# Pads in SBUF and three reorderings in a two-layer diffusion backbone

## The chip, the core and the metric

The kernel runs on one core of one Trainium2 chip, as one program. The metric is the device time of one execution in microseconds (us). The kernel before is known from three timed runs and from one more execution that was profiled.

## What is computed

The reference is one inference step of a hybrid backbone: two layers over 128 context tokens and 256 latent tokens of width 1024, all in float32. Each layer is a half-step SwiGLU FFN, a mixer, and a second half-step FFN.

```python
def _ffn_sublayer(x, shift, scale, gate, w1, w3, w2, g, b):
    y = _swiglu(_modulate(x, shift, scale), w1, w3, w2)
    return _layernorm(ALPHA * x + 0.5 * gate * y, g, b)
...
def _merge(h, y_f, y_m, y_n, p):
    g_f, g_m, g_n = jnp.split(jax.nn.sigmoid(h @ p['w_gate'] + p['b_gate']), 3, axis=-1)
    return (g_f * y_f + g_m * y_m + g_n * y_n) @ p['w_out']
```

The mixer projects the modulated input `h` by `w_in` into the inputs of three branches: a Fourier branch (`y_f`), latent attention (`y_m`) and neighbourhood attention (`y_n`). Beside the two token outputs the program returns the caches of the context tokens, among them the new neighbourhood keys (`new_na_k`) of both layers.

## The kernel before

**Numbers as pairs.** Every float32 operand of a product is held as a high and a low part in the reduced type fp32r, and `mm3` (line 327) issues three matmuls for each product: high by high, high by low, low by high. The weights come from HBM by SP's DMAs into `raw` tiles; ScalarE (ACT) casts them to `whi` (line 188) and VectorE (DVE) subtracts to get `wlo` (line 193).

**Memory.** There are two kinds of SBUF tiles. `fixed` tiles are placed once, in the order of the calls at the start of `run` (line 1231): the modulated activations `hm` (high part `hmh`, low part `hml`), the identity `ident`, and small ones. All larger working tiles are `slot`s, 26 of 4096 bytes and 22 of 3072 bytes to a partition, which stand behind the fixed tiles and are used again and again: `raw`, `whi`, `wlo`, the hidden activations `sT`, the queries and keys, the softmax rows `pr`, the residual rows `z`. Since 4096 and 3072 are multiples of 128, all slots start at one residue modulo 128 bytes.

**Stages.** The tokens are three tiles of 128. In an FFN `body` (line 1368) 22 hidden chunks `j` pass one after the other: for each, 48 matmuls of 384 columns make `w1` and `w3` (24 each; the profile calls both `w`), with weights as the stationary operand and `hm` as the moving one. Then 18 matmuls of 512 columns of `second` (line 1359) add an older chunk into the six output banks `y`; there the stationary operand is `sT` and the moving one a weight slot. The last eight chunks are kept for `tail` (line 1401), which adds them tile by tile, so that the layer norm of a tile (`residual`, line 538) goes on beside the matmuls of the next. The first chunks of the next stage (`head`: `hd` in an FFN; `uq`, `kv`, `uf` in a mixer) have `hm` as the stationary and the weights as the moving operand; so have the values `nv`.

**The mixer** (`mixer_body`, line 939) computes the neighbourhood queries and keys (`nq`, `nk`: weights stationary, `hm` moving, as in `w`), copies the context tokens' keys into `kf`, transposes these on TensorE into the bank `nkO`, copies that to `ko` and stores it from POOL's queue (lines 1142 to 1147). After that `attention` (line 846) runs over eight heads: scores `s` of two heads at a time, a filler piece (a gate chunk `g` of 24 matmuls and a branch chunk `yb` of 12), the transposes `pa` and `pb` of the head before, and the product with the values `o` (`attn_pv`, line 822) of the head before that.

**Order.** SP's queue is ordered by a planner from counted matmul columns. On the other engines the instructions follow the source within a scheduler's limits; each engine then runs its own queue in order and waits at semaphores.

The end of the program is the last call of `transition` (line 598): for the last tile the eight kept chunks are added to columns 0 to 511 and then to columns 512 to 1023; `residual` scales each half, adds `x`, takes the statistics, normalises and stores.

Of the kernel before, what the change touches and what calls it, by code (L numbers as in the profile page):

```python
# [8 lines left out]
F32 = mybir.dt.float32  # L9
F32R = mybir.dt.float32r  # L10
AF = mybir.ActivationFunctionType
ALU = mybir.AluOpType
# [4 lines left out]
P = 128  # L17
D = 1024
KD = 8
DEPTH = 2  # L20
NT = 3
TOK = 384
D_FF = 2816
NCH = D_FF // P
# [7 lines left out]
ALPHA = (2.0 * DEPTH) ** 0.25  # L32
# [56 lines left out]
class Kernel:  # L89
# [261 lines left out]
    def stats(self, x):  # L351
        nc = self.nc
        st = self.small(12)
        for h in range(2):
            nc.vector.bn_stats(out=st[:, h * 6:h * 6 + 6], in_=x[:, h * 512:h * 512 + 512])
        mv = self.small(2)
        nc.vector.bn_aggr(out=mv, in_=st.rearrange("p (a b) -> p a b", a=2))
        return mv


# [177 lines left out]
    def residual(self, t, ys, rows, f, last=None):  # L538
        nc = self.nc
        gate = rows[0 if t == 0 else 1]  # L540
        z = self.slot([P, D], F32, "z")
        sm = self.small(3)
        for h in range(2):
            c = slice(h * 512, h * 512 + 512)
            nc.vector.scalar_tensor_tensor(out=z[:, c], in0=ys[h], scalar=f, in1=gate[:, c], op0=ALU.mult, op1=ALU.mult)
            nc.vector.scalar_tensor_tensor(out=z[:, c], in0=self.x[t][:, c], scalar=ALPHA, in1=z[:, c], op0=ALU.mult, op1=ALU.add,
                                           accum_out=sm[:, h:h + 1])
        if last:
            mv = self.stats(z)
            r = self.rstd(mv[:, 1:2], 1.0, 1e-5)  # L550
            for h in range(2):
                c = slice(h * 512, h * 512 + 512)
                nc.vector.scalar_tensor_tensor(out=z[:, c], in0=z[:, c], scalar=mv[:, 0:1], in1=rows["ln_g"][:, c], op0=ALU.subtract, op1=ALU.mult)
            for h in range(2):
                c = slice(h * 512, h * 512 + 512)
                nc.vector.scalar_tensor_tensor(out=z[:, c], in0=z[:, c], scalar=r, in1=rows["ln_b"][:, c], op0=ALU.mult, op1=ALU.add)
                last(t, z, c)
            return
        st, _ = self.sumsq(z, sm[:, 0:1], sm[:, 1:2])
        r = self.rstd(st[:, 1:2], 1.0 / D, 1e-5)  # L560
        nc.vector.scalar_tensor_tensor(out=z, in0=z, scalar=st[:, 0:1], in1=rows["ln_g"], op0=ALU.add, op1=ALU.mult)
        nc.vector.scalar_tensor_tensor(out=z, in0=z, scalar=r, in1=rows["ln_b"], op0=ALU.mult, op1=ALU.add,
                                       accum_out=sm[:, 2:3])
        self.x[t], self.xsum[t] = z, sm[:, 2:3]
# [33 lines left out]
    def transition(self, prev, nxt, mod):  # L598
        n = {}
        if prev is None:  # L600
            with self.tc.manual_schedule(engines={mybir.EngineType.PE, mybir.EngineType.Activation, mybir.EngineType.DVE}):
                self.begin(nxt)
            return

        def res(t):
            self.residual(t, prev.ys[t], prev.rows(t), 0.5, prev.store if nxt is None else None)

        def norm(t):
            if nxt is not None:
                n[t] = self.normed(t)  # L610

        def modu(t):
            if nxt is not None:
                self.modulate(t, n.pop(t), self.mod[mod])

        tl = [prev.tail(t) for t in range(NT)]
        for p in tl[0]:
            p()
        res(0)
        norm(0)  # L620
        for p in tl[1]:
            p()
        cut = prev.cut
        if cut == 0:
            modu(0)
        a = self.ev
        res(1)
        for i, p in enumerate(tl[2]):
            if cut and i == cut:
                modu(0)  # L630
            p()
        norm(1)
        self.quiet.append((a, self.ev, HUSH[mod[1]] if mod else 0))
        if nxt is None:
            res(2)
            return
        late = LATE[mod[1]]

        def last():
            norm(2)  # L640
            if mod[1] == 1:
                for t in range(NT):
                    self.spill(mod[0], t)

        if late < 2:
            res(2)
        if late < 1:
            last()
        self.inhead = True
        hd = [nxt.head(t) for t in range(NT)]  # L650
        for t in range(2):
            at = (M1, M2)[t][mod[1]]
            for p in hd[t][:at]:
                p()
            modu(t + 1)
            if t == 0 and late > 1:
                res(2)
            if t == 0 and late > 0:
                last()
            for p in hd[t][at:]:  # L660
                p()
        for p in hd[2]:
            p()
        self.inhead = False
# [157 lines left out]
    def attn_pv(self, pt, v, h, oT):  # L822
        nc = self.nc
        o = self.psum("o")
        for oc, kts in ((slice(P, TOK), (1, 2, 3)), (slice(0, P), (0,))):
            for kt in kts:
                pc = slice(kt * 256 - 256, kt * 256) if kt else slice(768, 896)
                for y in range(2):
                    nc.tensor.matmul(o[:, oc], lhsT=v[kt][:, h].rearrange("p a b -> p (a b)"), rhs=pt[y][:, pc],
                                     start=kt == kts[0] and y == 0, stop=kt == kts[-1] and y == 1)  # L830
        if h % 2 == 0:
            self.oz = self.slot([P, TOK], F32, "oz")
        z = self.oz[h % 2 * 64:h % 2 * 64 + 64]
        nc.scalar.copy(out=z, in_=o[64:128, 0:TOK])
        nc.vector.tensor_tensor(out=z, in0=o[0:64, 0:TOK], in1=z, op=ALU.add)
        if h % 2:
            ot = self.slot([P, 2, TOK], F32R, "oT")
            self.split(ot[:, 0], ot[:, 1], self.oz)
            oT.append(ot)
# [99 lines left out]
    def mixer_body(self, ph):  # L939
        nc, I, K, O, l = self.nc, self.I, self.K, self.O, ph.l  # L940
# [91 lines left out]
        w = self.ukv(l, 0)  # L1032
        for pr in range(4):
            b = self.psum("kn")
            for kc in range(2):
                lhs = tuple(x[:, kc, 2 * pr:2 * pr + 2].rearrange("p a b -> p (a b)") for x in w)
# [5 lines left out]
        w = self.ukv(l, 1)  # L1042
        vm = []
        for t in range(4):
            b = self.psum("v")
# [35 lines left out]
        vn = []  # L1081
# [16 lines left out]
        oM = []  # L1098
# [25 lines left out]
        for p2 in range(4):  # L1124
            for nme in ("nq", "nk"):
# [10 lines left out]
                else:  # L1136
# [2 lines left out]
                    self.split(kk[:, 0, TOK:512], kk[:, 1, TOK:512], pk[:, p2 * P:(p2 + 1) * P])  # L1139
                    kN.append(kk)  # L1140
                    nc.vector.tensor_copy(out=kf[:, p2], in_=b[:, 0:P])
        po = self.psum("nkO")
        for p2 in range(4):
            nc.tensor.transpose(po[:, p2 * P:(p2 + 1) * P], kf[:, p2], self.ident)
        ko = self.slot([P, 512], F32, "ko")
        nc.scalar.copy(out=ko, in_=po)
        nc.gpsimd.dma_start(out=O[4][0, l].rearrange("a h j -> a (h j)"), in_=ko)

        early = {}

# [15 lines left out]
        def gate_early(d):  # L1166
            def go():
                early[d] = self.gate_chunk(l, 2, d, True)
            return go
# [9 lines left out]
            return x  # L1179

        oN = []
        self.attention(sc_na, 2, vn, oN, [acc_piece(1, d, oM) for d in range(KD)] + [gate_early(0), gate_early(1)])
        mT = []
        for d in range(KD):
            self.ada_flush()
# [45 lines left out]
    def run(self):  # L1231
        nc, I, K, O = self.nc, self.I, self.K, self.O

        self.hm = (self.fixed([P, KD, TOK], F32R, "hmh"), self.fixed([P, KD, TOK], F32R, "hml"))
        self.ident = self.fixed([P, P], F32, "ident")
        make_identity(nc, self.ident)
        self.mhalf = self.fixed([P, 1], F32, "mhalf")
        nc.vector.memset(self.mhalf, -0.5)
        self.mask = self.fixed([P, 64], F32, "mask")
# [38 lines left out]
class FFN:  # L1278
# [77 lines left out]
                k.split(st[:, 0], st[:, 1], b[:, 0:TOK])  # L1356
                self.sT[2 * g + a] = st

    def second(self, j, ts, start, stop, ns=range(2)):
        k = self.k  # L1360
        w2 = k.W(("w2", self.l, self.f, j), f"ffn{self.f}_w2", self.l, j * P, 1, 0, D)
        for t in ts:
            for n in ns:
                c = slice(n * 512, n * 512 + 512)
                lhs = tuple(self.sT[j][:, hl, t * P:(t + 1) * P] for hl in range(2))
                k.mm3(self.ys[t][n], lhs, tuple(w[:, 0, c] for w in w2), start, stop)

    def body(self):
        k, nc = self.k, self.k.nc
# [28 lines left out]
            self.second(q, range(NT), q == 0, False)  # L1398
        self.pend = pend

    def tail(self, t):
        def piece(j, ns):
            return lambda: self.second(j, [t], False, j == NCH - 1, ns)
        return [piece(j, [n]) for n in range(2) for j in self.pend]


class Mixer:
# [14 lines left out]
    def body(self):  # L1422
        self.k.mixer_body(self)

    def tail(self, t):
        k, l = self.k, self.l

        def piece(n, c):
            def go():
                if t not in self.ys:  # L1430
                    self.ys[t] = [k.psum("wo") for _ in range(2)]
                self.out(t, n, c)
            return go
        return [piece(n, c) for n in range(2) for c in range(KD)]
# [88 lines left out]
```

## Time and profile before

| quantity | value |
|---|---|
| median of 3 runs | 1880.86 us (1880.1 to 1881.82) |
| profiled execution | 1881.5 us |
| its span, first to last instruction | 1879.7 us |
| PE (TensorE) busy | 1853.3 us, 99% of the span |
| DVE busy | 1406.2 us, 75% |
| ACT busy | 786.9 us, 42% |
| POOL busy | 95.6 us, 5% |

The profiled execution lies 0.64 us over the median, and 1.8 us of it are outside the span. Matmuls are pipelined: the duration that the profile gives a single one (339 ns for one `w` of 384 columns) overlaps that of the next. The pace at which they follow each other is therefore read from a piece of the chain of waits, where so many matmuls of one kind stand with their common time: 48 in 8.48 us are 176.7 ns each. [...]

### The profile page before, as it was taken

How to read it: one execution, taken by the hardware profiler on the slowest of the kernel's cores; microseconds unless marked ns; L12 is line 12 of the kernel's file. 1: busy time of each engine (PE TensorE's matmuls, PEld its weight loads, DVE VectorE, ACT ScalarE, POOL GpSimd, SP SyncE). 2: the span in 40 equal slices, each digit the busy share in tenths (PEclk: the TensorE clock that was granted, in tenths of full speed). 3: DMA queues.
4: the chain of work that ended last, by engine and by line, in shares of the span. 5: the costliest groups of instructions: out<-in, count | busy, mean ns of one | idle time of the engine just before them, and what ended most of it. 6: DMA issues, size and time to landing. Idle time of an engine off the chain costs nothing. (4 is left out here: it accounts for less than half of the span.)

```text
span 1879.7 us, 27219 instructions
## 1 busy us (share of the span) xinstructions
PE 1853.3 (99%) x10555; PEld 1737.3 (92%) x10555; DVE 1406.2 (75%) x2190; ACT 786.9 (42%) x1312; POOL 95.6 (5%) x115
## 2 busy tenths in 40 slices
PE   7999999999999999999999999999999999999998
PEld 5899998999899999999999999999999998999996
DVE  5688888689887677888877878978798776533345
ACT  4433335456355453333353333355553553433330
POOL 0000002000100010000000000120001000000000
PEclk9999999999999999999999999999999999999999
DMA  9866656234735346666545666552365354344422
GB/s 302 279 217 211 211 201 212 88 100 125 226 106 196 123 146 217 197 224 210 193 150 189 223 215 214 191 163 88 113 197 152 112 194 138 118 134 123 145 91 79
DMA packets 225858, 320.22 MB, mean 170 GB/s; under 512 B 33040, under 2 KB 182144, under 8 KB 225600
## 3 DMA queue, kind: packets, MB, share of 16 engines
q1 hardware_dynamic: 223616, 313.89, 52.2%
q0 software_dynamic: 2112, 4.59, 0.6%
q8 instruction: 83, 1.36, 0.3%
q14 instruction: 47, 0.39, 0.1%
HBM read 312.32 MB, written 8.02 MB: 170 GB/s over the span
## 5 line engine op out<-in xcount | busy, mean ns | idle before, releaser
L193 DVE TENSOR_TENSOR wlo<-raw,whi 128x1024 fp32r<-128x1024 f32 (+4 forms) x420 | 490.6, 1185 | 156.2 <-ACT whi L188 73.9
L188 ACT CAST whi<-raw 128x1024 fp32r<-128x1024 f32 (+4 forms) x420 | 420.4, 1021 | 326.4 <-DVE wlo L193 83.7
L77 PE MATMUL w<-hmh,whi 128*128 128x384 f32 x1152 | 390.6, 339 | 0.8 <-ACT sl L77 0.8
L77 PE MATMUL w<-hmh,wlo 128*128 128x384 f32 x1152 | 389.6, 338 | 0.0
L77 PE MATMUL w<-hml,whi 128*128 128x384 f32 x1152 | 389.6, 338 | 0.0
L77 PE MATMUL y<-whi,sT 128*128 128x512 f32 x1056 | 336.7, 391 | 0.9 <-DVE sT L77 0.6
L77 DVE SCALAR_TENSOR_TENSOR acc<-raw,cs,acc 128x1024 f32<-128x1024 f32 x236 | 294.7, 1281 | 28.7 <-DMA raw<-in_w_ada_dram 28.5
L77 PEld LDWEIGHTS y<-whi,sT 128*128 128x128 f32 x1056 | 197.9, 188 | 40.6 <-DVE sT L77 1.2
L77 PEld LDWEIGHTS w<-hmh,whi 128*128 128x128 f32 x1152 | 216.3, 188 | 3.3 <-ACT sl L77 1.1
L77 PEld LDWEIGHTS w<-hml,whi 128*128 128x128 f32 x1152 | 216.2, 188 | 1.9
L77 PEld LDWEIGHTS w<-hmh,wlo 128*128 128x128 f32 x1152 | 216.2, 188 | 0.0
L77 PE MATMUL y<-wlo,sT 128*128 128x512 f32 x528 | 205.4, 390 | 0.0
L77 PE MATMUL g<-hmh,whi 128*128 128x384 f32 x384 | 132.0, 344 | 0.0
L77 PE MATMUL g<-hml,whi 128*128 128x384 f32 x384 | 129.3, 337 | 0.0
L77 PE MATMUL g<-hmh,wlo 128*128 128x384 f32 x384 | 129.2, 337 | 0.0
L77 PEld LDWEIGHTS y<-wlo,sT 128*128 128x128 f32 x528 | 99.1, 188 | 18.4
L77 ACT CAST sT<-sl 128x384 fp32r<-128x384 f32 x72 | 37.0, 514 | 187.6 <-DVE sl L77 187.6
L77 PE MATMUL hd<-whi,hmh 128*128 128x256 f32 (+1 forms) x336 | 100.6, 301 | 0.8 <-ACT hmh L77 0.7
L77 PE MATMUL hd<-wlo,hmh 128*128 128x256 f32 (+1 forms) x336 | 99.6, 298 | 0.0
L77 PE MATMUL hd<-whi,hml 128*128 128x256 f32 (+1 forms) x336 | 99.3, 298 | 0.0
L77 ACT ACTIVATE sl<-w 128x384 f32<-128x384 f32 x72 | 35.3, 490 | 115.4 <-PE w L77 115.4
L77 POOL TENSOR_TENSOR st<-st,mhalf 128x1 f32<-128x1 f32 x48 | 43.8, 914 | 703.1 <-DVE st L77 703.0
(263 smaller groups left out, 2968.0 us busy)
## 6 DMA issues: line engine op xcount, KB each, us to landing
raw<-in_ffn_w_dram SPq DMA_DIRECT2D x244, 512.0 KB, 4.7
raw<-in_w_ada_dram SPq DMA_DIRECT2D x128, 512.0 KB, 4.8
raw<-in_w_gate_dram SPq DMA_DIRECT2D x48, 512.0 KB, 4.6
raw<-in_w_in_dram SPq DMA_DIRECT2D x32, 512.0 KB, 6.6
raw<-in_w_out_dram SPq DMA_DIRECT2D x16, 512.0 KB, 6.4
raw<-gd SPq DMA_DIRECT2D x12, 512.0 KB, 5.8
raw<-in_ffn_w_dram SPq DMA_DIRECT2D x22, 256.0 KB, 5.2
raw<-in_ffn_w_dram SPq DMA_DIRECT2D x12, 384.0 KB, 8.7
```

Source lines behind the costliest of these rows:

```text
L77: r = f(*a, **kw)
L188: self.real.scalar.copy(out=hi, in_=r)
L193: self.real.vector.tensor_tensor(out=lo, in0=r, in1=hi.bitcast(F32), op=ALU.subtract)
```

## The change

It has four parts.

1. Two `fixed` tiles that nothing reads or writes, `pad`, stand ahead of `hm` (32 bytes) and behind `ident` (64 bytes). In the built programs the tiles then start at these bytes of each partition:

| tiles | start before | modulo 128 | start after | modulo 128 |
|---|---|---|---|---|
| `hmh` | 16512 | 0 | 16544 | 32 |
| `hml` | 28800 | 0 | 28832 | 32 |
| `ident` | 41088 | 0 | 41120 | 32 |
| first slot (and all others) | 43616 | 96 | 43712 | 64 |

A weight slot less `hm` is thus 96 modulo 128 before and 32 after; a slot less another slot is 0 in both. The residues modulo 512 behave alike: a slot less `hm` is 480 before and 32 after, and all parts of the operands that matmuls read lie multiples of 512 bytes apart, but for a few in the Fourier branch.

2. The transposes, the copy and the store of the new keys move into a function `new_keys` that runs behind the second filler piece of the neighbourhood attention.
3. `attn_pv` takes the high parts of the probabilities of all key tiles first, and then the low parts.
4. In the last tile the last three of the eight kept chunks are added to columns 512 to 767 and then to columns 768 to 1023, 256 columns at a time, and the last `residual` of every tile works in pieces of 512, 256 and 256 columns, with statistics of 256 columns.

```diff
@@ residual, when it is the last one
+            st = self.small(24, bufs=1)
+            for c0, n in ((0, 512), (512, 256), (768, 256)):
+                c = slice(c0, c0 + n)
+                nc.vector.scalar_tensor_tensor(out=z[:, c], in0=ys[c0 // 512][:, c0 % 512:c0 % 512 + n], scalar=f, in1=gate[:, c],
+                                               op0=ALU.mult, op1=ALU.mult)
+                nc.vector.scalar_tensor_tensor(out=z[:, c], in0=self.x[t][:, c], scalar=ALPHA, in1=z[:, c], op0=ALU.mult, op1=ALU.add)
+                for q in range(c0 // 256, (c0 + n) // 256):
+                    nc.vector.bn_stats(out=st[:, q * 6:q * 6 + 6], in_=z[:, q * 256:q * 256 + 256])
+            mv = self.moments(st, 4)
@@ attn_pv
-            for kt in kts:
-                pc = slice(kt * 256 - 256, kt * 256) if kt else slice(768, 896)
-                for y in range(2):
+            for y in range(2):
+                for kt in kts:
+                    pc = slice(kt * 256 - 256, kt * 256) if kt else slice(768, 896)
@@ mixer_body
+        def new_keys():
+            po = self.psum("nkO")
+            for p2 in range(4):
+                nc.tensor.transpose(po[:, p2 * P:(p2 + 1) * P], kf[:, p2], self.ident)
+            ko = self.slot([P, 512], F32, "ko")
+            nc.scalar.copy(out=ko, in_=po)
+            nc.gpsimd.dma_start(out=O[4][0, l].rearrange("a h j -> a (h j)"), in_=ko)
...
+        fill = [acc_piece(1, d, oM) for d in range(KD)] + [gate_early(0), gate_early(1)]
+        fill[1] = lambda go=fill[1]: (go(), new_keys())
+        self.attention(sc_na, 2, vn, oN, fill)
@@ run
+        self.fixed([P, 8], F32, "pad")
         self.hm = (self.fixed([P, KD, TOK], F32R, "hmh"), self.fixed([P, KD, TOK], F32R, "hml"))
         self.ident = self.fixed([P, P], F32, "ident")
         make_identity(nc, self.ident)
+        self.fixed([P, 16], F32, "pad")
@@ FFN.tail
+        a, b = self.pend[:-3], self.pend[-3:]
+        return ([piece(j, (0, 512)) for j in self.pend] + [piece(j, (512, 512)) for j in a] +
+                [piece(j, c) for c in ((512, 256), (768, 256)) for j in b])
```

**Two places in the order of the instructions.** The first is on PE in the first layer, where the neighbourhood attention begins; `kf` holds the copied keys, `s` are scores, `g` a gate chunk. In the kernel before, the first three transposes stand between the last `nk` and among the scores:

```order
L77 MATMUL nk_4952<-hmh_65,wlo_4772 128x384
L77 MATMUL nkO_4988<-ident_67,kf_4655 128x128 x2
L77 MATMUL s_937_4996<-kN_4734,qN_4694 128x384
L77 MATMUL s_939_4998<-kN_4734,qN_4694 128x384
L77 MATMUL nkO_4988<-ident_67,kf_4655 128x128
L77 MATMUL s_937_4996<-kN_4734,qN_4694 128x384
```

The fourth stands in the middle of the first gate chunk, also before the change:

```order
L77 MATMUL g_5055<-hml_66,whi_4888 128x384
L77 MATMUL g_5055<-hmh_65,wlo_4889 128x384
L77 MATMUL g_5055<-hmh_65,whi_4888 128x384
L77 MATMUL nkO_4988<-ident_67,kf_4655 128x128
L77 MATMUL g_5055<-hml_66,whi_4888 128x384
```

In the changed kernel the `nk` matmuls are followed by the scores at once, and PE's queue has all four transposes behind the second branch chunk, ahead of the transposes of the first head:

```order
L77 MATMUL yb_5136<-oT_4595,whi_4932 128x384 x2
L77 MATMUL yb_5136<-oT_4595,wlo_4933 128x384
L77 MATMUL nkO_5151<-ident_68,kf_4657 128x128 x4
L77 MATMUL pa_5159<-ident_68,pr_5013 128x128 x4
L77 MATMUL pb_5160<-ident_68,pr_5013 128x128 x2
```

So all four moved behind 72 matmuls of filler work. On POOL's queue the store of `ko` moved behind one addition of the bias mask; on ACT the copy of `ko` moved with the transposes.

The second place is DVE's queue at the end of the program, the last tile; the brackets show on which engine's semaphore an instruction waits. Before:

```order
L77 SCALAR_TENSOR_TENSOR z_17701<-y_15964,raw_17528 128x512 [waits PE_49]
L77 SCALAR_TENSOR_TENSOR z_17701,st_17702<-z_15474,z_17701 128x512 [waits DVE_49]
L77 BN_STATS st_17707<-z_17701 128x6 [waits DVE_49]
L77 SCALAR_TENSOR_TENSOR z_17701<-y_15965,raw_17528 128x512 [waits PE_49]
L77 SCALAR_TENSOR_TENSOR z_17701,st_17702<-z_15474,z_17701 128x512 [waits DVE_49]
L77 BN_STATS st_17707<-z_17701 128x6 [waits DVE_49]
L77 BN_AGGR st_17710<-st_17707 128x2 [waits DVE_49]
L77 TENSOR_SCALAR st_17712<-st_17710 128x1 [waits DVE_49]
```

After the change, with `y_15967` the bank of columns 512 to 1023:

```order
L77 SCALAR_TENSOR_TENSOR z_17718<-y_15966,raw_17530 128x512 [waits PE_49]
L77 SCALAR_TENSOR_TENSOR z_17718<-z_15476,z_17718 128x512 [waits DVE_49]
L77 BN_STATS st_17719<-z_17718 128x6 [waits DVE_49]
L77 BN_STATS st_17719<-z_17718 128x6
L77 SCALAR_TENSOR_TENSOR z_17718<-y_15967,raw_17530 128x256 [waits PE_49]
L77 SCALAR_TENSOR_TENSOR z_17718<-y_15967,raw_17530 128x256
L77 SCALAR_TENSOR_TENSOR z_17718<-z_15476,z_17718 128x256 [waits DVE_49] x2
L77 BN_STATS st_17719<-z_17718 128x6 [waits DVE_49] x2
L77 BN_AGGR st_17730<-st_17719 128x2 [waits DVE_49]
L77 TENSOR_SCALAR st_17732<-st_17730 128x1 [waits DVE_49]
```

Three steps over the second half became three pairs of steps over quarters. Of each pair that reads the bank only the first waits for PE. The value that it waits for is 10484, which PE's semaphore reaches with the last matmul of the program: the matmuls of both quarters of this bank count up together, by 33, at that one.

## Rows read from the trace of the kernel before

**Rows 1.** The page, part 1: busy time and share of the span by engine.

```profile
PE 1853.3 (99%) x10555; PEld 1737.3 (92%) x10555; DVE 1406.2 (75%) x2190; ACT 786.9 (42%) x1312; POOL 95.6 (5%) x115
```

**Rows 2.** Waits of PE for others: us in total, times, longest us.

```profile
PE nkO L77 <- DVE kf L77: 1.5, 2, 1.2
```

**Rows 3.** Windows by stage: length; busy us of PE, PEld, DVE, ACT, POOL; clock; DMA.

```profile
0.00:60.00 60.00, 50.23 (x286) 34.58 (x286) 34.25 (x89) 28.20 (x47) 4.03 (x12) 1.00 0.98 317
1000.00:1240.00 240.00, 240.00 (x1260) 224.32 (x1259) 201.69 (x233) 82.62 (x109) 11.84 (x16) 1.00 0.62 203
```

**Rows 4.** Windows of the `w` instructions alone: busy us (count) of PE, PEld, DVE, ACT.

```profile
75.00:290.00 215.00, 149.65 (x835) 146.87 (x833) 9.97 (x18) 8.35 (x17) 1.00 0.64 210
700.00:950.00 250.00, 155.19 (x864) 152.39 (x864) 9.96 (x18) 8.83 (x18) 1.00 0.60 199
1000.00:1240.00 240.00, 150.43 (x840) 147.74 (x840) 9.99 (x18) 8.36 (x17) 1.00 0.62 203
1640.00:1840.00 200.00, 147.72 (x825) 145.56 (x823) 9.99 (x18) 8.27 (x17) 1.00 0.41 124
```

**Rows 5.** Chain that ended last, an FFN body: start us, us, what, matmul count.

```profile
1001.05 8.48 PE w L77 x48
1009.53 4.08 PE y L77 x18
```

**Rows 6.** The same chain in the second mixer's neighbourhood projections and first heads.

```profile
1406.68 4.24 PE nk L77 x24
...
1432.27 4.18 PE nk L77 x24
...
1439.12 4.36 PE g L77 x24
...
1445.55 4.16 PE g L77 x24
1449.71 2.09 PE yb L77 x12
...
1452.57 1.52 PE s L77 x18
```

**Rows 7.** The same chain at the last FFN's head and its first body chunk.

```profile
1607.74 19.87 PE hd L77 x168
1627.61 4.16 PE w L77 x24
```

**Rows 8.** The same chain in the second mixer's head.

```profile
1245.36 5.59 PE uf L77 x24
...
1264.80 4.18 PE uq L77 x24
```

**Rows 9.** Timeline of PE, first layer's new keys: start us, us, instruction, idle before.

```profile
514.70 0.38 PE L77 MATMUL nkO<-ident,kf 128*128 128x128 f32 x2
...
517.34 0.45 PE L77 MATMUL g<-hmh,whi 128*128 128x384 f32 x1
...
518.48 0.34 PE L77 MATMUL g<-hmh,whi 128*128 128x384 f32 x1
520.05 0.33 PE L77 MATMUL nkO<-ident,kf 128*128 128x128 f32 x1 [1.23 <-DVE kf L77]
520.13 0.42 PE L77 MATMUL g<-hml,whi 128*128 128x384 f32 x1
```

**Rows 10.** Timeline of the program's end, DVE behind the last matmul.

```profile
1871.32 0.69 DVE L77 SCALAR_TENSOR_TENSOR z<-y,raw 128x512 f32<-128x512 f32 x1 [3.28 <-PE y L77]
...
1872.79 0.69 DVE L77 BATCH_NORM_STATS2 st<-z 128x6 f32<-128x512 f32 x1
...
1873.76 0.15 DVE L77 TENSOR_SCALAR st<-st 128x1 f32<-128x1 f32 x1
```

**Rows 11.** Groups by line and shape: count | busy us, mean ns | idle before.

```profile
L77 DVE TENSOR_TENSOR sf<-hd,sf 128x256 f32<-128x256 f32 x24 | 9.7, 420 | 11.6 <-ACT sf L77 11.6
```

More of the change, by code (lines that the diff above doesn't have):

```diff
@@ L355, in stats, with moments @@
             nc.vector.bn_stats(out=st[:, h * 6:h * 6 + 6], in_=x[:, h * 512:h * 512 + 512])
+        return self.moments(st, 2)
+    def moments(self, st, n):
         mv = self.small(2)
-        nc.vector.bn_aggr(out=mv, in_=st.rearrange("p (a b) -> p a b", a=2))
+        self.nc.vector.bn_aggr(out=mv, in_=st.rearrange("p (a b) -> p a b", a=n))
         return mv
@@ L541, in residual @@
         z = self.slot([P, D], F32, "z")
[L542 to L547, printed above, removed]
-        if last:
-            mv = self.stats(z)
+        if last:
+            st = self.small(24, bufs=1)
[7 more added lines that the diff above has]
+            mv = self.moments(st, 4)
             r = self.rstd(mv[:, 1:2], 1.0, 1e-5)
@@ L558, in residual @@
             return
+        sm = self.small(3)
+        for h in range(2):
+            c = slice(h * 512, h * 512 + 512)
+            nc.vector.scalar_tensor_tensor(out=z[:, c], in0=ys[h], scalar=f, in1=gate[:, c], op0=ALU.mult, op1=ALU.mult)
+            nc.vector.scalar_tensor_tensor(out=z[:, c], in0=self.x[t][:, c], scalar=ALPHA, in1=z[:, c], op0=ALU.mult, op1=ALU.add,
+                                           accum_out=sm[:, h:h + 1])
         st, _ = self.sumsq(z, sm[:, 0:1], sm[:, 1:2])
@@ L614, in modu @@
                 self.modulate(t, n.pop(t), self.mod[mod])
-        tl = [prev.tail(t) for t in range(NT)]
+        tl = [prev.tail(t, nxt is None and t == NT - 1) for t in range(NT)]
         for p in tl[0]:
@@ L1141, in mixer_body @@
                     nc.vector.tensor_copy(out=kf[:, p2], in_=b[:, 0:P])
[L1142 to L1147, printed above, removed]
+        def new_keys():
[5 more added lines that the diff above has]
+            nc.gpsimd.dma_start(out=O[4][0, l].rearrange("a h j -> a (h j)"), in_=ko)
         early = {}
@@ L1181, in mixer_body @@
         oN = []
-        self.attention(sc_na, 2, vn, oN, [acc_piece(1, d, oM) for d in range(KD)] + [gate_early(0), gate_early(1)])
+        fill = [acc_piece(1, d, oM) for d in range(KD)] + [gate_early(0), gate_early(1)]
+        fill[1] = lambda go=fill[1]: (go(), new_keys())
+        self.attention(sc_na, 2, vn, oN, fill)
         mT = []
@@ L1357, in head_finish, with second @@
                 self.sT[2 * g + a] = st
-    def second(self, j, ts, start, stop, ns=range(2)):
+    def second(self, j, ts, start, stop, cols=((0, 512), (512, 512))):
         k = self.k
@@ L1362, in second @@
         for t in ts:
-            for n in ns:
-                c = slice(n * 512, n * 512 + 512)
+            for c0, n in cols:
                 lhs = tuple(self.sT[j][:, hl, t * P:(t + 1) * P] for hl in range(2))
-                k.mm3(self.ys[t][n], lhs, tuple(w[:, 0, c] for w in w2), start, stop)
+                k.mm3(self.ys[t][c0 // 512][:, c0 % 512:c0 % 512 + n], lhs, tuple(w[:, 0, c0:c0 + n] for w in w2), start, stop)
     def body(self):
@@ L1399, in body, with tail, piece @@
         self.pend = pend
[L1401 to L1404, printed above, removed]
+    def tail(self, t, end=False):
+        def piece(j, c):
+            return lambda: self.second(j, [t], False, j == NCH - 1 and c != (512, 256), [c])
+        if not end:
+            return [piece(j, c) for c in ((0, 512), (512, 512)) for j in self.pend]
+        a, b = self.pend[:-3], self.pend[-3:]
+        return ([piece(j, (0, 512)) for j in self.pend] + [piece(j, (512, 512)) for j in a] +
+                [piece(j, c) for c in ((512, 256), (768, 256)) for j in b])
 class Mixer:
@@ L1423, in body, with tail @@
         self.k.mixer_body(self)
-    def tail(self, t):
+    def tail(self, t, end=False):
         k, l = self.k, self.l
```

## The prediction

> **What bounds the kernel now.** I read the busy shares first. PE is busy for 1853.3 of 1879.7 us, DVE for 75%, ACT for 42% [rows 1]. In an FFN body PE is busy for all of 240 us, DVE for 201.69 of them, and the DMA engines for 62% [rows 3]. So nearly everywhere the time is the number of matmuls times their pace, and another engine counts only where PE waits for it. The second view is the list of PE's waits: the only one that the change touches is that of the key transposes for DVE, 1.5 us [rows 2]. The third is the chain that ended last, for the pace.
>
> There the reader should see that one kind of matmul, with the same operands at the same addresses, has two paces. A run of 48 `w` takes 8.48 us, 176.7 ns each [rows 5]; 24 `w` behind the last head take 4.16 us, 173.3 ns each [rows 7]. `nk` is at 4.24 us for 24 early and at 4.18 us later; `g`, with the same two memory areas, is at 4.16 us [rows 6]. [...] `uq`, 384 columns with `hm` stationary, has 4.18 us for 24, 174.2 ns [rows 8]. `yb`, both operands in slots, has 2.09 us for 12, 174.2 ns [rows 6].
>
> [...]
>
> **Part 1, the pads.** They swap the sign of the distance between a slot and `hm`: stationary less moving was 96 for `w`, `g`, `nq`, `nk` and 32 for `uq`, `kv`, `uf`, `nv`, `hd`; now it is 32 and 96. For `y`, `wo`, `yb`, `q` it stays 0. The nearest row for `w` after the change is therefore `uq`, the same 384 columns at distance 32: 174.2 ns over a run whose first matmuls still settle. The best that any 384-column row shows is 173.3.
>
> How much `w` has to give: four windows hold 835 + 864 + 840 + 825 = 3364 of its 3456 matmuls in 149.65 + 155.19 + 150.43 + 147.72 = 602.99 us [rows 4]. Each of about 70 runs ends with a full duration of 0.34 us in place of its pace, 0.16 us too much, 11.4 us in all; 591.6 / 3364 = 175.9 ns. At 173.3 the gain is 2.6 x 3456 = 9.0 us, at 174.2 it is 1.7 x 3456 = 5.9 us. I take 8.2, near the upper end, because the excess of `uq` lies in the first matmuls of a run of 24 and most `w` runs are 48. `nq` and `nk` (384 matmuls) are slow in about six of eight runs a layer, `g` (1152) in about a third: 0.7 x 3.4 x 384 + 0.3 x 3.4 x 1152 = 0.9 + 1.2 = 2.1 us at most, 0.6 at `uq`'s pace; I take 1.3.
>
> The price: `uf` and `nv`, 288 matmuls of 512 columns, come to distance 96, for which no row has 512 columns. If they fall to `y`'s pace they give 6.2 x 288 = 1.8 us, if nothing changes 0; I take 0.9. `uq` (144) could take the slow pace, 2.5 x 144 = 0.4 us lost; I take 0.2. The 144 wide `hd` matmuls at the start run where the DMA engines are busy for 98% of 60 us [rows 3], and I count nothing for them. For the 864 `hd` of 256 columns (19.87 us for 168, 118.3 ns [rows 7]) and `kv` no second distance is known, and I count 0. The DMAs' targets move too; for the first 60 us I allow 1%, 0.6 us, either way. DVE's and ACT's operands shift as well, but PE covers them: DVE has 38 us to spare in 240 [rows 3].
>
> The rows show that the pace can differ by 6 ns between operands that all start at multiples of 32 bytes. [...]
>
> **Part 2, the new keys.** In the first layer the scores should take 1.52 us, as 18 of them do later [rows 6]. From the first transpose at 514.70 to the gate chunk at 517.34 are 2.64 us [rows 9]: 1.12 too many, of which three transposes are 0.33 (0.11 each). The fourth keeps the gate chunk from 518.48 to 520.13, 1.65 us for a step of 0.18 [rows 9]: 1.47 too many, 0.11 its own. So 0.79 + 1.36 = 2.1 us of waiting leave PE's path, and in the second layer 1439.12 - 1436.45 - 1.52 - 0.44 = 0.7 us [rows 6]. The transposes themselves remain, behind 72 matmuls that cover the copies they wait for. Their new neighbours wait behind them: `pa` on PE, needed for the first head, is 0.44 us later but 2 us earlier by the rest. ACT's copy and POOL's store go along, and no engine waits for the store; the next bias mask, queued behind it, is used a pair of heads later. What could be late instead is DVE, which was 4 us behind here. I take 2.6, with 1.5 and 2.8 as ends.
>
> **Part 3, the low parts.** The number of matmuls and weight loads is the same, and no wait for the low parts shows among PE's waits: 0.
>
> **Part 4, the last tile's end.** It should let DVE start on columns 512 to 767 while PE adds the last quarter. The order shows that it doesn't: the first step waits for the last matmul of the bank. So DVE's work behind the last matmul counts in full. Before, three steps of 512 columns from 1871.32 to the aggregate, 0.69 us each [rows 10]; now six of 256, of 0.42 us by the nearest row [rows 11]: 2.52 against 2.07, +0.45, less 0.08 for a read of the accumulator that goes. On PE 18 matmuls at 118.3 [rows 7] take the place of 9 at 226.7: 2.13 against 2.04, +0.09. The cost is 0.5 us, on the path, since nothing covers the end.
>
> **The sum.** 8.2 + 1.3 + 0.9 - 0.2 + 2.6 - 0.5 = 12.3 us less. The profiled execution's 1881.5 becomes 1869.2; it stood 0.6 over the median, so I predict 1868.6. All ends together: gains of 9.0 + 2.1 + 1.8 + 2.8 + 0.6 less 0.4 give 1865; 5.9 + 0.6 + 1.5 less 0.4, 0.6 and 0.6 give 1874.5.
>
> **Rivals.**
> - The pads do nothing: the pace of `w` is set by what ran before it and not by addresses. For it: `w` itself, at one address, is at 173.3 and at 176.7. Against it: `uf` and `y`, with the same columns, never meet. Then parts 2 and 4 remain, 2.1 us, 1878.8.
> - Slower: the residue itself counts, not the distance, and 64 is bad for two operands together. If `y` and `wo`, 1584 + 288 matmuls, take `uf`'s pace, that costs 6.2 x 1872 = 11.6 us. With `w` where it is, the time is 1880.9 + 11.6 - 2.1 = 1890.4. It decides from 1 ns on `y`: with `w` unchanged, 2.1 / 1872 = 1.1 ns eats up part 2. For it: no row has two operands at 64. Against it: shifted by the same amount, the two keep their distance.
> - Both: `w` gains and `y` loses, 1868.6 + 11.6 = 1880.2.
>
> **How the numbers follow.** About 0.2% (3.8 us) is what a measurement of this kernel can tell from no change. Forecast 0.62, all of it faster; pads that do nothing 0.19 and both 0.05, no change; slower 0.14. The range goes from 1864, a little under the ends' 1865, to 1880, which takes in the first rival and leaves out the slow one: about 0.8.
>
> **What would show it.** Right: `w` runs of 48 at 8.32 to 8.36 us, the gate chunk of the first layer without its gap, `y` still at 4.08 for 18, the aggregate 2.5 us behind the last matmul. Wrong: `w` still at 8.48 (first rival), or `y` at 4.2 for 18 (the slow one). If `w` is quick and the time isn't shorter, PE waits for DVE or the weights, and its list of waits must have grown.

## The result and the profile after

The changed kernel takes 1867.74 us in the median (1866.94 to 1868.0), the kernel before 1880.48 in the median of all its runs beside it: 0.9931 of it, with an interval from 0.992 to 0.9942. The forecast was 1868.6, in a range from 1864 to 1880. The profiled execution has 1866.1 us from the first to the last instruction, 13.6 less than before.

First the page, part 1, which answers to [rows 1]: busy time by engine.

```profile
PE 1842.0 (99%) x10564; PEld 1727.3 (93%) x10564; DVE 1401.2 (75%) x2196; ACT 787.5 (42%) x1312; POOL 94.4 (5%) x115
```

PE is busy for 11.3 us less, and its share of the span is what it was: the matmuls themselves became shorter. Where, the chain that ended last shows (start us, us, what, count of matmuls); it answers to [rows 5], [rows 7] and [rows 8].

```profile
993.34 8.32 PE w L77 x48
1001.66 4.08 PE y L77 x18
...
1227.53 4.24 PE uq L77 x24
...
1235.86 5.59 PE uf L77 x24
...
1255.34 4.16 PE uq L77 x24
...
1597.03 19.61 PE hd L77 x168
1616.64 4.16 PE w L77 x24
```

`w` fell from 8.48 to 8.32 us for 48, to 173.3 ns each. `y` and `uf` kept their paces. `uq` has runs at 4.24 beside runs at 4.16. `hd` of 256 columns, for which nothing was counted, went from 19.87 to 19.61 for 168. The windows of the `w` instructions alone say that nearly all of them are quick now (length, busy us and count of PE, PEld, DVE, ACT, then clock, DMA share and GB/s; the stretches are those of [rows 4], moved by what was gained ahead of them):

```profile
75.00:290.00 215.00, 146.75 (x832) 144.05 (x830) 9.97 (x18) 8.36 (x17) 1.00 0.64 214
695.00:945.00 250.00, 152.77 (x864) 150.04 (x864) 9.95 (x18) 8.83 (x18) 1.00 0.60 201
995.00:1235.00 240.00, 146.67 (x831) 143.84 (x829) 9.97 (x18) 8.37 (x17) 1.00 0.64 211
1630.00:1830.00 200.00, 144.01 (x819) 141.94 (x817) 10.00 (x18) 8.32 (x17) 1.00 0.42 127
```

590.20 us for 3346 are 176.39 ns, the last full duration of each run included, against 602.99 for 3364, 179.25 ns, in [rows 4]: 2.86 ns less, 9.9 us for all 3456. If the time from the start of each matmul to the start of the next is added up over the trace, `w` takes 9.6 us less, `hd` of 256 columns 1.3, `g`, `nq` and `nk` (without their waits and without the low clock described below) together 1.2; `yb` takes 0.5 more, `uq` and `kv` 0.4.

The second gain is at the new keys. The chain of after in the first and then the second layer:

```profile
513.02 1.55 PE s L77 x18
514.57 4.36 PE g L77 x24
518.93 2.10 PE yb L77 x12
521.04 4.17 PE g L77 x24
525.21 2.11 PE yb L77 x12
527.32 0.44 PE nkO L77 x4
...
1426.30 1.55 PE s L77 x18
...
1440.60 0.44 PE nkO L77 x4
```

From the end of `nk` to the end of the transposes are 527.76 - 513.02 = 14.74 us in the first layer and 1441.04 - 1426.30 = 14.74 in the second. Before, the same work ran from 514.70 [rows 9] to the first `pa` at 531.51, 16.81 us, and from 1436.44 [rows 6] to 1451.80, 15.36. So 2.07 and 0.62 us went, 2.7 together. The wait for `kf` is gone from PE's list of waits.

What was not forecast stands a little earlier in the first layer. PE waits there for DVE's `red`, before as after; then the `nq` behind it run slowly:

```profile
484.75 0.69 PE ada L77 x2
485.44 6.78 PE nq L77 x24
492.22 4.16 PE nk L77 x24
```

24 `nq` take 6.78 us in place of 4.16. The granted clock of the stretch is 0.65 of full speed (481.2 to 491), and 0.50 in its part from 486 to 490 us. There the `nq` start 0.32 us apart; from 491 to 495, at a clock of 1.00, matmuls of the same 384 columns start 0.17 us apart. Before, the same stretch had 0.79 (484 to 492), and the `nq` took 1.0 us less by their starts.

At the end of the program the steps of DVE behind the last matmul, which answer to [rows 10]:

```profile
1857.43 0.28 PE L77 MATMUL y<-whi,sT 128*128 128x256 f32 x1
1857.74 0.76 DVE L77 SCALAR_TENSOR_TENSOR z<-y,raw 128x256 f32<-128x256 f32 x2 [3.35 <-PE y L77]
1858.42 0.75 DVE L77 SCALAR_TENSOR_TENSOR z<-z,z 128x256 f32<-128x256 f32 x2
1859.09 0.74 DVE L77 BATCH_NORM_STATS2 st<-z 128x6 f32<-128x256 f32 x2
1859.87 0.26 DVE L77 BATCH_NORM_AGGREGATE st<-st 128x2 f32<-128x24 f32 x1
```

DVE waits 3.35 us and begins behind the last matmul, as the order of the instructions had said. But two steps of 256 columns in a row take 0.76 us together, where one of 512 took 0.69, and the next pair begins 0.67 to 0.78 us after the one before. From DVE's first step to the aggregate are 2.13 us; before they were 2.19 (from 1871.32 to 1873.51).

### The profile page after: what moved, and what is told of

Read it like the earlier page. It is cut to its first block, busy times and chain, and to the rows that moved or that the text cites. A ratio compares the mean times of both kernels' runs of the same rounds, so it can differ in the third digit from the quotient of the medians.

```text
span 1866.1 us, 27248 instructions
## 1 busy us (share of the span) xinstructions
PE 1842.0 (99%) x10564; PEld 1727.3 (93%) x10564; DVE 1401.2 (75%) x2196; ACT 787.5 (42%) x1312; POOL 94.4 (5%) x115
## 4 chain that ended last, share of the span: by engine, by line
PE 96%; DVE 2%; ACT 1%; issue 0%; DMA 0%; SPq 0%; DVEq 0%
PE w L77 32%; PE y L77 19%; PE g L77 11%; PE hd L77 7%; PE yb L77 5%; PE wo L77 4%; PE nq L77 2%; PE s L77 2%; PE nv L77 2%; PE uf L77 2%; PE nk L77 2%; PE o L77 1%; PE uq L77 1%; DVE k L77 1%; PE kv L77 1%; PE q L77 1%
## 5 line engine op out<-in xcount | busy, mean ns | idle before, releaser
L77 PE MATMUL y<-whi,sT 128*128 128x512 f32 (+1 forms) x1062 | 336.7, 389 | 0.3 <-ACT sT L77 0.2
```

The source lines that it names most:

```text
L77: r = f(*a, **kw)
```

## The experiments

The theory: the two pads carry 10 us through the pace of the matmuls, which depends on the distance between the two operands' addresses; the new keys carry 2.7; the rest is nothing. Rivals: the order around the matmuls sets the pace; or the residue of one memory area does, and not a distance.

**The pads alone.** The kernel before with one edit:

```
+        self.fixed([P, 8], F32, "pad")
         self.hm = ...
         make_identity(nc, self.ident)
+        self.fixed([P, 16], F32, "pad")
```

> The kernel before with the two pads alone: hm at 32 and the slots at 64 modulo 128; the order of the instructions is that of before. If the pads carry the gain, as the sum of the prediction has it, nearly all w runs of 48 fall from 8.48 to 8.32-8.34 us, hd of 256 columns goes from 118.3 to 116.7 ns, and the time is 10 to 11.5 us under the kernel before (1869 to 1870.5). Rival: the paces changed in the trace of after because the order of the work changed around them, not because of the pads; then w stays at 8.48 for 48 and the time is within 1.5 us of before (1879 to 1881.5).

Measured: 1870.65 us (1869.64 to 1871.83), 0.9945 of before, interval 0.9931 to 0.9959: 10.1 us less. The chain:

```profile
996.61 8.32 PE w L77 x48
```

PE's waits for DVE grew by 1.1 us at two places (`nkO` 2.0 in place of 1.5, one `y` 1.2 in place of 0.6). So the paces come from the pads, and a tenth of what they give runs into DVE.

**Both areas moved alike.** Only the pad ahead of `hm`: `hm` at 32, the slots at 0.

> The kernel before with only the pad ahead of hm: hm at 32 and the slots at 0 modulo 128. Both areas are shifted by the same 32 bytes, so the distance of a weight slot to hm stays at 96 modulo 128, as in the kernel before. If the distance sets the pace, everything is as before: w 8.48 us for 48, hd of 256 columns 118.3 ns, time 1880 to 1881. Rival, the residue of hm itself counts (0 is bad, 32 is good): w takes 8.32 us for 48 as in the changed kernel and the time is 1869 to 1871. Rival, the residue of the slots counts (96 is bad): the same, 1869 to 1871, and y may move too.

Measured: 1881.06 us (1880.02 to 1881.44), ratio 1.0001, interval 0.9992 to 1.001. The chain:

```profile
999.69 8.48 PE w L77 x48
```

Every residue changed and the pace didn't: what counts is the distance.

**Distance 0.** Only a pad of 32 bytes behind `ident`.

> The kernel before with only a pad of 32 bytes behind ident: hm at 0 and the slots at 0 modulo 128, distance 0 for all pairs of operands. If the distance sets the pace, w, g, nq, nk take what yb takes at distance 0, 173.3 to 174.9 ns (8.32 to 8.40 us for 48); uf, nv and the first hd, 432 matmuls of 512 columns, fall from 233.3 to the 226.7 ns of y, 2.9 us less; hd of 256 columns goes from 118.3 to about 119 (the o matmuls' pace), 0.6 us more. Sum: 6.5 to 9.6 less for w, 1.2 for g, nq, nk, 2.9 less, 0.6 more: 10 to 13 us under before, 1867.5 to 1870.5. Rival, the residue of hm counts (0 is bad): w stays at 176.7, time 1879 to 1881.

Measured: 1873.23 us (1871.91 to 1874.69), 0.9961, interval 0.9948 to 0.9973. Its chain, at the same places as above:

```profile
998.27 8.34 PE w L77 x48
1006.62 4.12 PE y L77 x18
...
1241.37 5.48 PE uf L77 x24
...
1602.46 20.15 PE hd L77 x168
```

`w` and `uf` came about as expected (`uf` 228.3 ns and not 226.7). The miss is `hd`, 119.9 ns, 1.9 us more over its 864 matmuls by the starts, and `y`, whose own two operands lie no differently: 4.12 for 18, 1.9 us more in all (waits left out of both). No distance is best for all kinds.

**The new keys alone**, without pads:

```
+        def new_keys():
+            po = self.psum("nkO")
...
+        fill[1] = lambda go=fill[1]: (go(), new_keys())
```

> The kernel before with the new keys in a function behind the second filler piece, and nothing else. If the waits for kf were worth what the prediction has for them, the stretch from the last nk to the first pa is 2.1 us shorter in the first layer and 0.6 in the second, as in the trace of after, and the time is 2.7 us under before (1877.5 to 1878.3); w stays at 8.48 for 48. Rival: part of it is given back later, since PE then meets DVE earlier; then the stretch is as short but the time is less than 1.5 us under before.

Measured: 1877.74 us (1876.98 to 1880.13), 0.9985, interval 0.9977 to 0.9994: 3.0 us less, as expected. From the end of the last `nk` to the end of the transposes are 14.7 us in both layers. With the 10.1 of the pads that is 13.1, and the changed kernel has 12.7: nothing is left over for the low parts and the end.

**Other distances.** First a distance of 160 (a pad of 192 bytes behind `ident`), then 64 (96 bytes), `hm` at its old place in both.

> The kernel before with hm left at 0 and a pad of 192 bytes behind ident: slots at 32 modulo 128. The distance of a weight slot to hm is 32 modulo 128 as in the changed kernel, but with other residues (0 and 32 in place of 32 and 64), and 160 in place of 32 modulo 512. If the distance modulo 128 alone sets the pace, w is at 8.32-8.34 us for 48, hd of 256 columns at 116.7 ns, uf at 233.3, and the time equals that of the pads alone, 1870.6 within 1 us. Rival, the distance counts modulo 256 or 512: the paces differ from those of the pads alone, w may be anywhere between 173.3 and 176.8, time up to 1881.

Measured: 1887.95 us (1887.22 to 1889.22), 1.0039, interval 1.0026 to 1.0052. The chain:

```profile
1004.13 7.95 PE w L77 x45
...
1249.47 5.62 PE uf L77 x24
...
1613.49 16.62 PE hd L77 x140
```

`w` is at 176.7 ns, and in this kernel in every one of its 144 runs of 24. Against the trace of before `w` takes 1.5 us more by the starts, `y` 1.6 and `g`, which has no quick run left, 2.4. The prediction's own picture, a distance modulo 128, gave 1870.6 here: it fell by 17 us.

> The kernel before with hm left at 0 and a pad of 96 bytes behind ident: slots at 64 modulo 128, the distance is 64 both ways, which no kernel here has had. Three distances are known: 96 (w 176, hd of 256 columns 116.7, uf 233), 32 (w 173.4, hd 118.3, uf 233), 0 (w 173.7, hd 119.9, uf 228). If the pace changes smoothly with the distance, 64 lies between 32 and 96: w 174.7, uf 233, hd 117.5, and the time is 1874 to 1877. Rival: 64 is as good as 0 or better for 512 columns, since the two streams are then farthest apart: uf near 227, w 173.4, time 1867 to 1870.

Measured: 1880.91 us (1880.18 to 1881.85), ratio 1.0, interval 0.9991 to 1.0009. `w` 8.48 for 48, `uf` 5.51 for 24 (229.6), `hd` 19.79 for 168 (117.8). Neither guess held: `uf` is nearly as good as at distance 0, and `w` as bad as in the kernel before. PE also waits 2.3 us for `kf`.

**Which residue, which period.** Again slots at 32 and `hm` at 0, but with 64 bytes of pad behind `ident` in place of 192; and the pads of the change with the tile `mask` placed ahead of `hm`, which moves `hm` by another 256 bytes.

> The kernel before with hm left at 0 and a pad of 64 bytes behind ident: slots at 32 modulo 128, and a weight slot less hm is 32 also modulo 512. The kernel with 192 bytes there had the same residues modulo 128 (0 and 32) but 160 modulo 512, and all its w runs were slow (176.7). If the distance counts over more than 128 bytes, this one has the paces of the pads alone: w 8.32-8.34 us for 48, hd of 256 columns 116.7, uf 233, time 1870.6 within 1 us. Rival, the two residues modulo 128 count (0 and 32 are a bad pair, 32 and 64 a good one): w at 176.7, time 1888 as with 192 bytes.

Measured: 1870.77 us (1870.17 to 1871.73), 0.9945, interval 0.9932 to 0.9957; the chain:

```profile
995.61 8.33 PE w L77 x48
...
1238.11 5.60 PE uf L77 x24
...
1600.01 19.61 PE hd L77 x168
```

> The pads alone, and in addition the tile mask (256 bytes) placed ahead of hm instead of behind ident. hm moves by 256 bytes and the slots stay, so a weight slot less hm is 32 modulo 256 as in the changed kernel, but 288 modulo 512. If the pattern repeats every 256 bytes, the paces and the time are those of the pads alone, 1870.6. If it repeats every 512 or more, the distance is one that no kernel here has had, and w can be anywhere between 173.3 and 176.8, time 1869 to 1888.

Measured: 1871.61 us (1870.31 to 1872.08), 0.9947, interval 0.9933 to 0.996; the chain:

```profile
996.72 8.32 PE w L77 x48
```

Distances 32 and 288 give the same paces, 160 others. So the distance counts over more than 128 bytes, and these kernels agree with a period of 256. They show it for one pair of distances only.

| weight slot less `hm`, modulo 512 | `w`, 48 | `uf`, 24 | `hd`, each | time with that alone |
|---|---|---|---|---|
| 480 (before) | 8.48, some runs of 24 at 4.16 | 5.59 | 118.3 ns | 1880.5 |
| 0 | 8.34 | 5.48 | 119.9 | 1873.2 |
| 32 (the change's pads) | 8.32 | 5.59 | 116.7 | 1870.7 |
| 64 | 8.48, some runs of 24 quicker | 5.51 | 117.8 | 1880.9 |
| 160 | 8.48 (7.95 for 45) | 5.62 | 118.7 | 1888.0 |

**The end.** The changed kernel without its last part (`residual` and `tail` as before).

> The changed kernel with the last tile's end as before (chunks of 512 columns, statistics of 512); pads, new keys and low parts stay. By the prediction the end's pieces of 256 cost 0.5 us, so this is 1867.2. By the trace of the changed kernel they cost nothing: from the start of the last matmul to the end are 8.67 us against 8.80 before, and 18 matmuls of 256 take 2.15 us where 9 of 512 took 2.04; then it is 1867.7 to 1867.8.

Measured: 1867.9 us (1867.43 to 1869.44), where the changed kernel has 1867.74: the pieces of 256 columns cost nothing and bring nothing.

**The wait for `red`, later.** The changed kernel with the placing matmul due one step later:

```
-        self.ada_due.append([2, lambda: self.ada_place(blk, red)])
+        self.ada_due.append([3, lambda: self.ada_place(blk, red)])
```

> The changed kernel with the matmul that places a conditioning block (ada) due three steps after its reduction instead of two, everywhere. In the first layer PE waits 3.4 us for DVE there, and the nq behind it run at a lower granted clock (24 in 6.78 us in place of 4.16). If that wait is what drops the clock, both go: 3.4 + 2.6 = 6.0 us less, 1861.7. Rival: DVE is behind by more than one step and the wait only moves to the next place, 1867 to 1868; or a conditioning block comes too late for a layer norm or a gate's row, then PE has a new wait elsewhere.

Measured: 1869.43 us (1867.87 to 1869.88), 1.7 more than the changed kernel. The waits of PE (us in total, times, longest us):

```profile
PE g L77 <- DVE qN L77: 1.7, 1, 1.7
PE g L77 <- DVE wlo L193: 1.6, 1, 1.6
```

The wait at `nq` is gone and stands, with 3.3 us, at a gate chunk, and the clock falls there instead (0.97 from 513 to 550 us): the rival. DVE is behind in this stretch, and moving the one instruction that meets it helps nothing.

**Fewer steps for DVE there, twice.** First four of the conditioning steps taken from the mixer's account and put on that of the FFN ahead of it:

```
-        budget = {(0, 0): 36, (0, 1): 12, ...
+        budget = {(0, 0): 40, (0, 1): 8, ...
```

> The changed kernel with four of the conditioning steps (ada) of the first mixer moved into the FFN before it: 40 and 8 steps instead of 36 and 12; the second layer has 8 in its mixer already. If DVE is late at the first layer's nq because of these steps (two additions of about 1.25 us each), PE's wait of 3.4 us for red goes, the nq behind it keep the full clock (2.6 us), and no wait takes its place: 1867.7 - 6.0 = 1861.7. Rival: DVE's ten more us in the FFN make PE wait there, or the mixer's wait only moves as it did with the later due step: 1866 to 1870.

Measured: 1883.36 us (1882.03 to 1885.94), 15.6 more than the changed kernel. One row of PE's waits, and DVE's `acc` steps in the windows from 480 to 600 and from 600 to 660 (length; busy us and count of DVE, of POOL; clock, DMA share, GB/s):

```profile
PE ada L77 <- DVE red L77: 16.5, 2, 13.1
480.00:600.00 120.00, 10.97 (x9) 0.00 (x0) 0.97 0.42 122
600.00:660.00 60.00, 12.26 (x10) 2.81 (x4) 0.89 0.52 177
```

The FFN has no place for four more steps: of its 22 chunks four are made in the head as `hd`, and only the 18 that make `w` in the body spend steps, two each, so that 36 was already all of them (the count of `acc` instructions from 55 to 270 us, 76, is that of the changed kernel). So they were caught up at the mixer's end, ten `acc` instructions between 600 and 660 us, and PE waited 13.1 us. The edit did not do what it was for. Then the same four steps spread by hand:

```
                 for nme in ("nq", "nk"):
-                self.ada_spend(1)
+                if nme == "nq":
+                    self.ada_spend(1)
...
+        for i in (3, 6):
+            fill[i] = lambda go=fill[i]: (self.ada_spend(1), go())
...
-            self.ada_flush()
+            self.ada_spend(1 if d in (0, 2) else 0)
```

> The changed kernel with the four conditioning steps that stand ahead of the neighbourhood keys moved: two into filler pieces of the neighbourhood attention (the fourth and the seventh), two ahead of the last branch's first and third chunk. Eight additions of DVE, 10 us, leave the stretch in which PE waits for it, and the placing matmul comes 48 matmuls (8.3 us) later. The later due step alone removed the nq wait but PE then waited 3.3 us for DVE (qN, wlo) at the gate chunk, and moving all four to the mixer's end cost 13 us of waiting there. If DVE's backlog in this stretch is the cause, neither wait appears, PE keeps the full clock, and the time is 1867.7 - 6.0 = 1861.7. Rival: the attention and the last branch have less room on DVE than their 5 to 9 us of idle time in 37 to 50 us suggest, and PE waits there: 1866 to 1870.

Measured: 1862.96 us (1861.39 to 1865.17), 0.9911 of before, interval 0.9894 to 0.9927: 4.8 us under the changed kernel, of the 6.0 expected, and the quickest of all. The intervals of the two ratios overlap; the slowest of its four runs (1865.17) is still under the quickest of the changed kernel (1866.94). The wait for `red` is gone from PE's list, and no new one has taken its place. The stretch from 450 to 660 us (busy us of PE, PEld, DVE, ACT, POOL; clock, DMA share, GB/s), first in this kernel and then in the changed one:

```profile
450.00:660.00 210.00, 210.00 (x1236) 199.93 (x1235) 179.51 (x334) 103.44 (x195) 15.76 (x13) 1.00 0.54 165
```

```profile
450.00:660.00 210.00, 206.20 (x1205) 196.83 (x1204) 168.39 (x320) 98.26 (x185) 16.20 (x12) 0.98 0.53 165
```

PE has no gap and keeps the full clock: 31 matmuls more fit into the same 210 us.

## Why the prediction came out right, and where its steps did not

- **What bounds the kernel.** Right: PE is at 99% before and after, and of the 13.6 us between the two profiled executions 11.3 are less busy time of PE.
- **`w`, 8.2 taken, 5.9 to 9.0.** 9.6 by the starts, 9.9 by the windows: above the range. The nearest row was right in kind and `w` did go to 173.3 ns; the term that was too small is its pace before. The 0.16 us taken off for the end of each run put it at 175.9 ns, and the run of [rows 5] itself says 176.7.
- **`g`, `nq`, `nk`, 1.3.** 1.2. Right in the total. The count of slow `nq` and `nk` runs, six of eight a layer, holds for the second layer; in the first only the two runs ahead of the wait for `red` were slow.
- **`uf`, `nv`, 0.9.** 0: still 5.59 for 24. The 6.2 ns in the sum are the 232.9 ns of `uf` [rows 8] less the 226.7 ns of `y` [rows 5]. The step that failed is that another distance would bring them toward `y`. By the table `uf` is slow at 480, at 32 and at 160 (5.59 to 5.62 us for 24), and quicker only at 0 (5.48) and 64 (5.51).
- **`uq`, 0.2 lost.** Measured with `kv` together, 0.4. Two of the six `uq` runs went to 176.7 ns throughout, two more in part.
- **`hd` of 256 columns, `kv` and the pairs of slots, nothing.** `hd` gave 1.3 and `yb` took 0.5. `yb` shows that a pair whose own distance is unchanged can change pace; so does `y` at distance 0. By the starts only the first matmuls of such a run differ: five or six of a `yb` run take 172 to 185 ns, nine or ten of a `y` run 224 to 236, and the rest are at 173.4 and 226.7 as in other runs.
- **The DMA engines, 0.6 either way.** The first wait for a DMA is 7.9 us before and 7.6 after, 7.6 to 8.0 in all kernels: nothing that the runs tie to the pads.
- **The new keys, 2.6.** 2.7 in the two stretches. The kernel with them alone took 3.0 less.
- **The low parts, 0.** Not run alone; the pads' and keys' gains leave nothing for them.
- **The end, 0.5 lost.** 0. That it would not overlap was right. The price of a step was wrong: 0.42 us is one step's duration, and two in a row cost 0.76 and not 0.84 and overlap the next pair, so that six took 2.13 where 2.52 were set down.
- **Not in the sum:** the low clock behind the wait for `red`, 1.0 us lost in the profiled execution. The wait itself is 3.3 to 3.4 us in every kernel that has it, but the 24 `nq` behind it then lose between 1.6 and 2.7 us by their starts (0.1 in the one with distance 64, whose clock falls only behind its wait for `kf`, 0.66 from 515 to 520 us). The kernel before lost 1.6, the changed kernel 2.7 and the changed kernel without its end, alike up to there, 1.7: no pattern goes with an edit, and why it varies is open.
- **The sum.** 9.6 + 1.2 + 1.3 - 0.5 - 0.4 + 2.7 - 1.0 = 12.9. The two profiled executions are 13.6 us apart, the medians 12.7; a wait at a `y` (0.5) and the first wait for a DMA (0.3), both shorter in the changed kernel's trace, make up the rest of the 13.6. That the forecast of 12.3 is so near is partly luck: the gains of `w` and `hd` were 2.7 us too low and the end 0.5 too dear, while `uf`, `yb` and the clock were set 2.4 us too well.
- **The rivals.** Pads that do nothing: `w` at 8.32 with the pads alone rules it out as the main cause. A part of it is true, as the next point says: at distance 480 the share of slow `w` runs of 24 is 125 of 144 in the trace of before and 111 of 144 in two kernels with the same distance, a difference of 1.1 us. Slower by the residue of two slots: `y` stayed at 4.08, and a shift of both areas changed nothing. But a slower kernel by pads was near: 128 bytes more between the areas give 1888.0.
- **What went before.** In the trace of before the state of a `w` run goes with what stands directly ahead of it; `ada` are the two short placing matmuls:

```profile
1051.29 0.17 PE ada L77 x2
1051.46 8.38 PE w L77 x48
1059.83 4.13 PE y L77 x18
1063.96 8.48 PE w L77 x48
```

  All 49 runs of 24 that begin behind 18 `y` are slow, all 81 that follow another run of `w` keep its state, and seven of the nine behind `ada` are quick; but the `y` behind a quick run take 4.13 us in place of 4.08, which gives half of it back. In the two other kernels at 480 and in the one at 64 (where the quicker runs are at about 174.8) the counts are 49 of 49, 81 of 81 and nine of nine. At 32 all 144 runs are quick and at 160 all are slow, whatever stands ahead. These are counts by the starts; no run at these distances moved an `ada` to test it.
- **The picture behind it.** The text speaks of residues modulo 128. That was too coarse: two kernels with the same residues modulo 128, at distances 32 and 160, take 1870.77 and 1887.95 us, 17.2 us apart.

## What to carry to other kernels

Where PE is busy nearly always (99% of the span here), compare the paces of matmuls of equal columns. Here `w` stood at 176.7 and at 173.3 ns, and `uf` and `y` at 232.9 and 226.7; that made the place of one operand against the other worth trying, and two pads of one line each gave 10.1 us. Try a few distances on the chip and count every kind of matmul, since no distance here was the best for all, and what a new distance did to `uf`, `hd` and `yb` could not have been told from the rows of before. After that look at what PE meets next: here DVE's backlog cost more than the 3.4 us of the wait, because the clock fell behind it (0.65 from 481.2 to 491 us), and spreading DVE's work gave 4.8 us where moving the waiting instruction gained nothing (1869.43 us against 1867.74).

## What the runs showed of the hardware

- In these kernels the pace of a matmul with its weight load depends on the distance of its two operands in SBUF: 384 columns take from 173.3 to 176.7 ns, 512 from 226.7 to 234 ns, 256 from 116.7 to 119.9 ns. Shifting both areas by 32 bytes left 48 `w` at 8.48 us and the time at 1881.06; distances 32 and 288 were alike (8.33 and 8.32 us for 48 `w`), 32 and 160 were not (160: 7.95 us for 45, 8.48 for 48 at that pace).
- The roles count too: at 32 `w`, with the weights stationary, is quick, and two of six runs of `uq`, with the same areas in exchanged roles, are slow (176.7) throughout; at 480 it is `w` that is slow, and no run of `uq` stays slow (24 in 4.17 to 4.18 us). In both cases the slow one has its stationary operand 480 ahead of its moving one, modulo 512.
- At distances 480 and 64 the pace of `w` has two states (176.7 and 173.3 ns at 480, 176.7 and about 174.8 at 64). It stays in one for a whole run of 24 or 48 matmuls, and into the next run when that follows directly (81 of 81); behind 18 `y` it was the slow one each time (49 of 49).
- After 3.4 us of waiting, 24 `nq` took 6.78 us, with a granted clock of 0.65 from 481.2 to 491 us; without the wait (the kernel with the spread steps) the clock is 1.00 from 470 to 500 us.
- Two DVE steps of 256 columns in a row take 0.76 us, one takes 0.42 by [rows 11], and one of 512 takes 0.69.
